# Retention's values and keys through small tiles while attention's room is taken

## The chip, the cores and the metric

The kernel runs on one core of a Trainium2 chip. The metric is the device time of one execution in microseconds (us). The core has a matrix engine (TensorE, PE in the profile; its weight loads stand apart as PEld), VectorE (DVE), ScalarE (ACT), GpSimd (POOL) and a queue that issues transfers (SyncE, SP). Each takes its instructions in the order in which they were written; semaphores tie them together.

## The reference

Two layers of a diffusion backbone over 1024 latent tokens and 256 context tokens, width 1024. What matters of a layer:

```python
h, gate_lat = modulate(x, norm_gain[i], cond_lat @ w_mod[i] + b_mod[i])
(a_uv, a_g, r_q, r_k, r_v, r_g, g_q, g_k, g_v, g_g, s_q, s_k, s_v, s_g) = split_columns(h @ w_in[i])
mlp_l = chunk_mlp_branch(a_uv, a_g, mlp_mix[i], mlp_bias[i])
ry_l, _, _ = retention_bidir(to_heads(r_q), to_heads(r_k) * k_scale, to_heads(r_v), lg_f, lg_b, st_f, st_b)
ret_l = from_heads(rms_norm(ry_l, ret_gain)) * jax.nn.silu(r_g)
ga_l = from_heads(blocked_attention(...)) * jax.nn.silu(g_g)
swa_l = from_heads(window_attention(...)) * jax.nn.silu(s_g)
x = x + gate_lat * (jnp.concatenate([mlp_l, ret_l, ga_l, swa_l], axis=-1) @ w_out[i])
```

Retention works in chunks of 128 tokens: `kv` is the product of decayed keys and values of a chunk, a scan over the chunks makes states of it, and each output is a product inside the chunk plus one with the state before it. The context tokens (two of the ten chunks) go through the same weights, in the second layer only where the latent tokens need them.

## The kernel before, in words

The input projection of a layer is cut into 13 groups of 256 columns, in the order C0, gg, C1, sg, D0, v, D1, ua0, Bv, Bk, Bb0, Bb1, ua1: C and D make queries, keys and values of the two attentions (global and windowed), gg and sg their gates, v and ua the MLP's parts, Bv and Bk retention's values and keys, Bb0 and Bb1 its queries and gates. Four groups of the output projection follow. A group is made of units. `unit_a` (L429) makes two chunks of tokens by 256 columns in 48 matmuls, `unit_b` (L443) 128 columns by four chunks in 24 matmuls of 512 or by two chunks in 24 of 256 (fp32 in three passes of two rounded halves). Each unit writes one PSUM tile of the tag `pj`, of which there are two: a unit can start only when the unit before the last one has been evacuated.

Everything else is hung between the units. While the program is built, a planner keeps a modelled clock of every engine. A step is put down with `later(fn, need, when)`: it is written into the queues when its time has come by the model, when the tiles it needs will be free within 300 ns (`fits`), and when its condition `when` holds. Steps with matmuls come through `pe`. Attention runs as jobs from a list (`attend`, `scores`), at most three in flight: S = q k (L974), the row maximum (DVE, L993), exp (ACT, L1015), a split into two fp16 halves (ACT L1023, DVE and POOL L1032), two transposing DMAs (L1029, L1035), the product with the values (L1045), a sum into M (L1057, L1061), and at the end of a chunk of four token blocks `norm`, which takes a tile of the tag `gd` for the gate and needs it before M can go. When a unit finds no free `pj`, the planner goes on writing only jobs and steps until one comes free (`room`, `until`).

Pools of tiles (`BUFS`, `ATT`): `gd` has 4 tiles of 128x512 f32. Its users near the change are the gate `gt` of an attention chunk and `tab`, the constants for retention's decay tables (`decay_tables`, loaded at L695 and last read at L715). `qkt` has 2 large tiles. They hold the queries and keys of an attention group until the scores of all its jobs are written, and afterwards retention's values (`vt`) and keys (`kT`).

In `ret_v_group` each of the five units of Bv is evacuated by ScalarE into its part of `vt` (L1275). The first of these evacuations waits for a `qkt` tile, the others until that one has taken it. In `ret_k_group` the six units of Bk, two of 256 and four of 512 columns, are evacuated into `kT` with the factor 0.125 (L1293), again the first one waiting for `qkt`. Each is then turned by TensorE into a `pm` tile (`turn`, ktp at L579), scaled by the decay into `kf` (L1314 and L1316, which need `PT` tiles: all three for the first, since two become the states), multiplied with the values (kvp, L1330) and scanned (L1363). Bb0 and Bb1 then make queries and gates; `ready` (sc, L1386) waits until the scan of its half is done and the decay tables are there; `outs` (y, L1414, L1418) follows.

Of the kernel before, what the change touches and what calls it, by code (L numbers as in the profile page):

```python
# [12 lines left out]
F32 = mybir.dt.float32  # L13
# [3 lines left out]
AF = mybir.ActivationFunctionType  # L17
# [5 lines left out]
NT = 10  # L23
# [15 lines left out]
LOOK = 300.0  # L39
# [151 lines left out]
class Program:  # L191
# [161 lines left out]
    def room(self, need):  # L353
        self.until(lambda: self.fits([(need, 1)], None))
# [914 lines left out]

    def ret_v_group(self, W, st):  # L1270

        def keep(pair, ps):
            if "v" not in st:
                st["v"] = self.tile(self.ap, (128, NT, 256), F32, "qkt", "vt")
            self.S.activation(st["v"][:, 2 * pair:2 * pair + 2, :].rearrange("p t c -> p (t c)"), ps, AF.Copy)  # L1275
            self.done(ps)
            st["values"] = st.get("values", 0) + 1

        for pair in (4, 0, 1, 2, 3):
            ps = self.unit_a(W, pair, last=pair == 3)  # L1280
            self.later(lambda pair=pair, ps=ps: keep(pair, ps), "qkt" if pair == 4 else "", None if pair == 4 else lambda: "v" in st)

    def ret_k_group(self, W, st):
        V, S, T, lc = self.V, self.S, self.T, self.lc[self.l]

        kvs, sts = {}, {}
        st["st"], st["S"] = sts, set()

        def get(p, ch, ps):
            t0, n = CHUNKS[ch]  # L1290
            if "k" not in st:
                st["k"] = self.tile(self.ap, (128, 2, NT * 128), F32, "qkt", "kT")
            S.activation(st["k"][:, p, 128 * t0:128 * (t0 + n)], ps[:, :128 * n], AF.Copy, scale=0.125)  # L1293
            self.done(ps)
            self.pe(lambda: turn(p, ch))

        def turn(p, ch):
            t0, n = CHUNKS[ch]
            pk = self.pm("ktp")
            self.turn(pk, st["k"][:, p, 128 * t0:128 * (t0 + n)], n, "k")  # L1300
            first = not st.get("turned")
            st["turned"] = True
            self.later(lambda: scale(p, ch, pk), "PT:3" if first else "PT", None if first else lambda: len(sts) == 2)

        def scale(p, ch, pk):

            n = CHUNKS[ch][1]
            pkv = pk[:, :128 * n].rearrange("p (t h d) -> p t h d", h=2, d=64)
            if not sts:

                for q in range(2):
                    sts[q] = self.tile(self.ap, (128, NT, 2, 64), F32, "PT", "st")
            kf = self.tile(self.ap, (128, 2, 4, 2, 64), F32, "PT", "kf")
            V.tensor_mul(kf[:, 0, :n], pkv, lc["kd"][:, 0, 2 * p:2 * p + 2].unsqueeze(1).unsqueeze(3).to_broadcast([128, n, 2, 64]))  # L1314
            for h in range(2):
                S.activation(kf[:, 1, :n, h, :], pkv[:, :, h, :], AF.Identity, scale=lc["kd"][:, 1, 2 * p + h:2 * p + h + 1], bias=self.zero)  # L1316
            self.done(pk)
            self.pe(lambda: products(p, ch, kf), "pm", lambda: st.get("values") == 5)

        def products(p, ch, kf):  # L1320
            t0, n = CHUNKS[ch]
            vt = st["v"]
            po = self.pm("kvp")
            for i in range(n):
                for fb in range(2):
                    o = 128 * i + 64 * fb

                    for h in range(2):
                        c = 128 * p + 64 * h
                        T.matmul(po[64 * h:64 * h + 64, o:o + 64], kf[:, fb, i, h, :], vt[:, t0 + i, c:c + 64], start=True, stop=True)  # L1330
            self.done(kf)
            self.later(lambda: keep(p, ch, po), "P" if ch == 2 else "", None if ch == 2 else lambda: p in kvs and (p, ch - 1) in kvs)

        fs, bs = [8, 9, 0, 1, 2, 3, 4, 5, 6, 7], [9, 8, 7, 6, 5, 4, 3, 2, 1, 0]

        def keep(p, ch, po):
            t0, n = CHUNKS[ch]
            if ch == 2:
                kvs[p] = self.tile(self.ap, (128, NT, 2, 64), F32, "P", "kv")
                kvs[p, -1] = True  # L1340
            kvs[p, ch] = True
            S.activation(kvs[p][:, t0:t0 + n].rearrange("p t f d -> p (t f d)"), po[:, :128 * n], AF.Copy)
            self.done(po)
            if ch == 2:
                V.memset(sts[p][:, 8, 0], 0.0)
                V.memset(sts[p][:, 9, 1], 0.0)
                scan(p, range(0, 2), range(0, 2))
            elif ch == 0:
                scan(p, range(2, 6), ())
            else:  # L1350
                scan(p, range(6, 9), range(2, 5))
                self.later(lambda: end(p))

        def end(p):
            scan(p, (), range(5, 9))
            self.done(kvs[p])
            self.later(lambda: st["S"].add(p))

        def scan(p, fwd, bwd):
            steps = [(0, fs[s], fs[s + 1]) for s in fwd], [(1, bs[s], bs[s + 1]) for s in bwd]  # L1360
            both = [x for i in range(max(map(len, steps))) for y in steps for x in y[i:i + 1]]
            for fb, a, b in both:
                V.scalar_tensor_tensor(sts[p][:, b, fb, :], sts[p][:, a, fb, :], lc["cd"][:, 2 * p + fb:2 * p + fb + 1],  # L1363
                                       kvs[p][:, a, fb, :], ALU.mult, ALU.add)

        for ch in (2, 0, 1):
            for p in range(2):
                ps = self.unit_b(W, p, ch, p == 1 and ch == 1)
                self.later(lambda p=p, ch=ch, ps=ps: get(p, ch, ps), "qkt" if (p, ch) == (0, 2) else "", None if (p, ch) == (0, 2) else lambda: "k" in st)

    def ret_out_group(self, W, p, st):
        V, S, G, T, lc = self.V, self.S, self.G, self.T, self.lc[self.l]
# [422 lines left out]
```

## Time and profile before

| | us |
|---|---|
| three runs, median | 1315.66 |
| lowest, highest | 1308.14, 1317.33 |
| the profiled execution's own time | 1318.18 |
| its span, first to last instruction | 1316.4 |
| mean granted clock of TensorE, as a share of full speed | 0.987 |

In the windows view a row gives, for one stretch of the span (us from its start), its length, then for PE, PEld, DVE, ACT and POOL the busy time and the number of instructions, then the clock granted to TensorE as a share of full speed, the share of the DMA engines and GB/s. What a PE's busy time leaves of the length is idle. In the timeline a row gives start, duration, engine, line, operation, output and inputs, shape and count; a bracket at its end holds the idle time before it and what ended that. The tile view gives duration as least, median and greatest in ns and the first and last start in us.

### The profile page before, as it was taken

Reading aid. Unit: us, or ns where it says so; the run is one execution under the profiler, and the core shown is the slowest. Engines: PE = TensorE matmul, PEld = TensorE weight load, DVE = VectorE, ACT = ScalarE, POOL = GpSimd, SP = SyncE. Lnnn points to the kernel's source line nnn. Section 1 sums busy time; section 2 is a strip of 40 time slices with the busy share of each in tenths; the row PEclk is TensorE's granted clock in tenths of the full one; section 3 lists DMA queues with packets and bytes.
Section 4 is the critical chain, followed back from the end, with each engine's and each line's share of the span. In section 5 each row is a group of like instructions: output and inputs, shape, how many; then the busy total and the mean of one; then the engine's idle time right before and its main releaser. Section 6 shows DMA issues by size and latency. Waiting matters only on the chain.

```text
span 1316.4 us, 27946 instructions
## 1 busy us (share of the span) xinstructions
PE 1272.4 (97%) x10720; PEld 1121.9 (85%) x10720; DVE 841.8 (64%) x2022; ACT 703.4 (53%) x1467; POOL 610.6 (46%) x616
## 2 busy tenths in 40 slices
PE   6989999999999899999999999999999889999998
PEld 4877878889989788888999978789888778888998
DVE  4765878888897734237225957778898884523522
ACT  3555768777776831235224647667778674213210
POOL 2585855835843213234112486769486422323320
PEclk9999999999999999999999999999999999988999
DMA  9426899799789922163612257997988985105531
GB/s 365 151 77 153 136 203 214 145 201 204 146 164 192 213 75 69 45 190 115 216 33 99 90 142 145 193 196 134 189 170 156 198 162 117 40 21 196 181 112 49
DMA packets 373351, 194.13 MB, mean 147 GB/s; under 512 B 303297, under 2 KB 333665, under 8 KB 372193
## 3 DMA queue, kind: packets, MB, share of 16 engines
q1 hardware_dynamic: 373072, 192.28, 62.6%
q8 instruction: 84, 1.38, 0.4%
q14 instruction: 51, 0.41, 0.1%
q10 hardware_dynamic: 144, 0.07, 0.0%
HBM read 94.63 MB, written 23.74 MB: 90 GB/s over the span
## 4 chain that ended last, share of the span: by engine, by line
PE 79%; DVE 9%; POOL 3%; ACT 3%; issue 3%; DMA 3%; SPq 1%; POOLq 0%; ACTq 0%; DVEq 0%
PE ua L429 32%; PE ub L443 26%; PE S L974 6%; PE O L1045 5%; DVE P L993 2%; PE y L1418 2%; PE y L1414 2%; PE mod L520 1%; POOL rr L567 1%; DMA xt<-in_x 1%; PE u L1714 1%; PE kvp L1330 1%; PE sc L1386 1%; DVE qr L827 1%; DVE L L1032 1%
## 5 line engine op out<-in xcount | busy, mean ns | idle before, releaser
L429 PE MATMUL ua<-w,HT 128*128 128x256 f32 x4128 | 525.2, 285 | 0.4 <-ACT vt L1275 0.4
L429 PEld LDWEIGHTS ua<-w,HT 128*128 128x128 f32 x4128 | 502.8, 191 | 3.8 <-issue 1.7
L443 PE MATMUL ub<-HT,w 128*128 128x512 f32 (+1 forms) x1824 | 402.8, 374 | 4.8 <-ACT kT L1293 2.5
L443 PEld LDWEIGHTS ub<-HT,w 128*128 128x128 f32 x1824 | 311.7, 193 | 63.3 <-ACT kT L1293 3.3
L372 POOL TENSOR_TENSOR w<-raw,w 128x512 fp32r<-128x512 f32 x132 | 185.1, 1413 | 269.3 <-ACT w L370 240.2
L1032 DVE TENSOR_TENSOR L<-P,H 128x1120 f16<-128x1120 f32 (+2 forms) x104 | 143.1, 1376 | 18.2 <-ACT H L1023 16.8
L370 ACT ACTIVATE w<-raw 128x512 fp32r<-128x512 f32 x136 | 83.3, 625 | 109.1 <-PE ua L429 49.2
L993 DVE CUSTOM_DVE_ANT_0 P<-S,zero 128x512 f32<-128x512 f32 (+2 forms) x216 | 116.1, 581 | 29.7 <-PE S L974 14.0
L974 PE MATMUL S<-qkt 128*128 128x256 f16 (+2 forms) x768 | 124.7, 304 | 4.1 <-DVE mx L993 4.1
L1032 POOL TENSOR_TENSOR L<-P,H 128x160 f16<-128x160 f32 (+2 forms) x104 | 81.3, 782 | 97.2 <-ACT H L1023 65.0
L1023 ACT ACTIVATE H<-P 128x1280 f16<-128x1280 f32 (+2 forms) x104 | 124.5, 1197 | 2.1 <-DMA PT<-H 1.2
L1015 ACT ACTIVATE P<-P,mx,gmxC 128x1280 f32<-128x1280 f32 (+1 forms) x72 | 97.5, 1354 | 17.7 <-DVE mx L1002 16.6
L1045 PE MATMUL O<-vh,PT 128*128 128x128 f16 (+1 forms) x1952 | 101.8, 207 | 4.3 <-DVE M L1061 3.1
L974 PEld LDWEIGHTS <-qkt 128*128 128x128 f16 x768 | 64.5, 98 | 45.5 <-issue 7.6
L1045 PEld LDWEIGHTS <-PT 128*128 128x128 f16 x1952 | 88.2, 98 | 14.4 <-issue 8.0
L1598 DVE TENSOR_TENSOR tm<-ua,gb 128x512 f32<-128x512 f32 (+1 forms) x37 | 24.9, 674 | 114.5 <-PE ua L429 114.5
L573 ACT ACTIVATE ev<-ub 128x512 f32<-128x512 f32 (+1 forms) x64 | 34.7, 542 | 110.0 <-PE ub L443 89.7
L567 POOL TENSOR_TENSOR rr<-rt,mhalf 128x6 f32<-128x6 f32 (+3 forms) x60 | 76.2, 1269 | 5.0
L1015 ACT ACTIVATE P<-P,mx,gmxD 128x640 f32<-128x640 f32 (+2 forms) x72 | 61.4, 853 | 16.9 <-DVE mx L1006 12.5
L1121 DVE SCALAR_TENSOR_TENSOR sl<-th,ev 128x512 f32<-128x512 f32 (+1 forms) x40 | 34.4, 860 | 34.5 <-ACT th L1116 32.9
L993 DVE CUSTOM_DVE_ANT_0 P<-S,mask 128x512 f32<-128x512 f32 (+2 forms) x112 | 50.5, 483 | 8.1 <-PE S L974 5.4
L827 POOL TENSOR_TENSOR rt<-sw,cst 128x192 f32<-128x192 f32 x64 | 49.2, 789 | 3.0 <-ACT sw L833 2.6
(177 smaller groups left out, 1547.0 us busy)
## 6 DMA issues: line engine op xcount, KB each, us to landing
raw<-in_win SPq DMA_DIRECT2D x104, 256.0 KB
raw<-in_wmod SPq DMA_DIRECT2D x64, 256.0 KB
wm<-in_wmod SPq DMA_DIRECT2D x8, 1024.0 KB
raw<-in_wout SPq DMA_DIRECT2D x32, 256.0 KB
xt<-in_x SPq DMA_DIRECT2D x4, 1024.0 KB
silu<-sl SPq DMA_DIRECT2D x16, 256.0 KB
gt<-silu SPq DMA_DIRECT2D x16, 256.0 KB
mxd<-mg SPq DMA_DIRECT2D x16, 256.0 KB
```

The source lines that it names most:

```text
L370: self.S.activation(w[:, :, 0, :], rv, AF.Copy)
L372: self.e(f"w{'i' if o < 0 else 'to'[o > 0]}low{q}").tensor_sub(w[:, :, 1, :], rv, w[:, :, 0, :].bitcast(F32))
L429: self.T.matmul(ps[:, 256 * i:256 * i + 256], self.HT[:, 2 * pair + i, k, sa, :], W[k // 2][:, k % 2, sb, :], start=(j == 0 and n == 0), s ...
L443: self.T.matmul(ps[:, :128 * n], W[k // 2][:, k % 2, sa, 128 * b:128 * b + 128], self.HT[:, t0:t0 + n, k, sb, :], start=(k == 0 and m == 0 ...
L567: self.G.tensor_tensor(r[:, :n], t[:, :n], self.mhalf[:, :n], ALU.pow)
L827: E.tensor_mul(out[:, :, :, 32 * c:32 * c + 32], x[:, :, :, 32 * c:32 * c + 32], t.to_broadcast([128, 2, 3, 32]))
L974: T.matmul(sp[o // 4][:, c:c + 128 * m], qk[:, t, heads[s], :], qk[:, keys[i]:keys[i] + m, b, :], start=(b == 2), stop=(b == 3))
L993: V.tensor_tensor_reduce(out=P[:, 128 * o:128 * (o + m)], in0=sp[o // 4][:, c:c + 128 * m], in1=mk, scale=1.0, scalar=-3e38, op0=ALU.add, ...
L1015: S.activation(P[:, ws * s:ws * s + ws], P[:, ws * s:ws * s + ws], AF.Exp, scale=lc["c"][typ][0], bias=mx[:, s:s + 1], accum_out=sv[:, col ...
L1023: S.activation(H[:, 0:w], P[:, 0:w], AF.Copy)
L1032: E.tensor_sub(L[:, a:b], P[:, a:b], H[:, a:b])
L1045: T.matmul(O[:, 128 * s:128 * s + m], pt[:, pl * len(cols) + j, :], vh()[:, kt, 0:m], start=(j % nk == 0 and pl == 0), stop=(j % nk == nk ...
```

## The change

Both groups now ask for their `qkt` tile at once, in a step of its own (`room`). A unit that is done before the tile is there may be evacuated into a `gd` tile ("wait"), if at least two of the four are free at that moment (`spare`); GpSimd then copies it to its place once the large tile has been taken, and frees the small one. Only then does the evacuation count as done: for the values in `st["values"]`, for the keys by starting `turn`. `turn` has a new condition besides: the first waits until three `PT` tiles are free, the others until the states have taken theirs.

```diff
     def ret_v_group(self, W, st):
+        def room():
+            st["v"] = self.tile(self.ap, (128, NT, 256), F32, "qkt", "vt")
+
         def keep(pair, ps):
-            if "v" not in st:
-                st["v"] = self.tile(self.ap, (128, NT, 256), F32, "qkt", "vt")
-            self.S.activation(st["v"][:, 2 * pair:2 * pair + 2, :].rearrange("p t c -> p (t c)"), ps, AF.Copy)
-            self.done(ps)
+            self.evac_or_move(ps, 512, lambda: st["v"][:, 2 * pair:2 * pair + 2, :].rearrange("p t c -> p (t c)"), "v" in st, lambda: "v" in st, 1.0, over)
+
+        def over(src):
             st["values"] = st.get("values", 0) + 1
 
+        self.later(room, "qkt")
         for pair in (4, 0, 1, 2, 3):
             ps = self.unit_a(W, pair, last=pair == 3)
-            self.later(lambda pair=pair, ps=ps: keep(pair, ps), "qkt" if pair == 4 else "", None if pair == 4 else lambda: "v" in st)
+            self.later(lambda pair=pair, ps=ps: keep(pair, ps), "", lambda: "v" in st or self.spare())
+
+    def spare(self):
+        return sum(r <= self.now + LOOK for r in self.slots["gd"]) >= 2
+
+    def evac_or_move(self, ps, n, dst, now, there, factor, then):
+        if now:
+            self.S.activation(dst(), ps[:, :n], AF.Copy, scale=factor)
+            self.done(ps)
+            then(dst())
+            return
+        x = self.gd(n="wait")
+        self.S.activation(x[:, :n], ps[:, :n], AF.Copy, scale=factor)
+        self.done(ps)
+
+        def move():
+            self.G.tensor_copy(dst(), x[:, :n])
+            self.done(x)
+            then(dst())
+
+        self.later(move, "", there)
 
     def ret_k_group(self, W, st):
...
         def get(p, ch, ps):
             t0, n = CHUNKS[ch]
-            if "k" not in st:
-                st["k"] = self.tile(self.ap, (128, 2, NT * 128), F32, "qkt", "kT")
-            S.activation(st["k"][:, p, 128 * t0:128 * (t0 + n)], ps[:, :128 * n], AF.Copy, scale=0.125)
-            self.done(ps)
-            self.pe(lambda: turn(p, ch))
+            self.evac_or_move(ps, 128 * n, lambda: st["k"][:, p, 128 * t0:128 * (t0 + n)], "k" in st, lambda: "k" in st, 0.125,
+                              lambda src: self.pe(lambda: turn(p, ch), "pm", lambda: len(sts) == 2 or not st.get("turned") and self.fits([("PT", 3)], None)))
+
+        def room():
+            st["k"] = self.tile(self.ap, (128, 2, NT * 128), F32, "qkt", "kT")
...
+        self.later(room, "qkt", lambda: "v" in st)
         for ch in (2, 0, 1):
             for p in range(2):
                 ps = self.unit_b(W, p, ch, p == 1 and ch == 1)
-                self.later(lambda p=p, ch=ch, ps=ps: get(p, ch, ps), "qkt" if (p, ch) == (0, 2) else "", None if (p, ch) == (0, 2) else lambda: "k" in st)
+                self.later(lambda p=p, ch=ch, ps=ps: get(p, ch, ps), "", lambda: "k" in st or self.spare())
```

## Rows read from the trace of the kernel before

**Rows 1.** The page's first part: busy time, share of the span, instructions.

```profile
PE 1272.4 (97%) x10720; PEld 1121.9 (85%) x10720; DVE 841.8 (64%) x2022; ACT 703.4 (53%) x1467; POOL 610.6 (46%) x616
```

**Rows 2.** Windows view, the three stretches without projection matmuls and what follows two.

```profile
435.90:448.12 12.22, 7.83 (x104) 5.97 (x101) 10.75 (x41) 10.91 (x26) 2.76 (x5) 1.00 0.95 217
448.12:452.45 4.33, 4.33 (x31) 3.65 (x31) 3.22 (x10) 3.11 (x9) 0.71 (x2) 0.61 0.99 236
1026.13:1039.17 13.04, 8.19 (x111) 6.66 (x109) 11.23 (x40) 9.82 (x25) 4.20 (x5) 1.00 1.04 208
1072.45:1082.97 10.52, 6.92 (x67) 4.90 (x65) 9.96 (x32) 7.23 (x17) 3.83 (x5) 0.84 0.76 157
1082.97:1088.34 5.37, 5.37 (x33) 4.16 (x33) 3.09 (x15) 3.65 (x9) 0.00 (x0) 0.68 0.49 91
```

**Rows 3.** Timeline of PE, layer 0, group Bk.

```profile
435.90 2.36 PE L974 MATMUL S<-qkt 128*128 128x256 f16 x24
...
448.12 2.93 PE L443 MATMUL ub<-HT,w 128*128 128x512 f32 x6 [2.04 <-ACT kT L1293]
...
452.45 1.63 PE L443 MATMUL ub<-HT,w 128*128 128x512 f32 x6
```

**Rows 4.** Timeline of PE, layer 1, group Bv.

```profile
1021.74 4.55 PE L429 MATMUL ua<-w,HT 128*128 128x256 f32 x36
...
1032.61 1.01 PE L1045 MATMUL O<-vh,PT 128*128 128x128 f16 x20 [1.64 <-DVE M L1061]
...
1039.17 3.02 PE L429 MATMUL ua<-w,HT 128*128 128x256 f32 x23 [0.42 <-ACT vt L1275]
```

**Rows 5.** Timeline of PE, layer 1: a block's scores earlier, then group Bk.

```profile
1042.15 1.05 PE L974 MATMUL S<-qkt 128*128 128x256 f16 x8
...
1072.45 2.40 PE L974 MATMUL S<-qkt 128*128 128x256 f16 x24
...
1080.61 1.89 PE L974 MATMUL S<-qkt 128*128 128x256 f16 x8 [0.68 <-DVE mx L993]
1082.97 2.93 PE L443 MATMUL ub<-HT,w 128*128 128x512 f32 x6 [0.47 <-ACT kT L1293]
```

**Rows 6.** Windows view, the long stretches behind the retention groups' start.

```profile
452.45:700.00 247.55, 246.99 (x1931) 221.50 (x1929) 95.11 (x187) 79.64 (x202) 71.86 (x62) 0.99 0.35 107
1090.00:1310.00 220.00, 219.09 (x1649) 196.06 (x1648) 84.30 (x152) 55.33 (x110) 59.41 (x48) 0.97 0.35 106
```

**Rows 7.** Timeline of PE, whole units run together (48 matmuls of 256, 24 of 512).

```profile
1014.20 5.99 PE L429 MATMUL ua<-w,HT 128*128 128x256 f32 x48
...
1138.79 5.75 PE L443 MATMUL ub<-HT,w 128*128 128x512 f32 x24
...
1173.38 8.16 PE L443 MATMUL ub<-HT,w 128*128 128x512 f32 x24
```

**Rows 8.** Decay constants' tile tab in layer 1, tile view: its load, its last reader.

```profile
L715 ACT ACTIVATE qd<-tab,lconst x4: 385/386/386, 1074.8 to 1075.7; 128x128 f32<-128x128 f32 x4
L695 SPq DMA_DIRECT2D tab<-in_consts x1: 570/570/570, 1056.9 to 1056.9; - x1
```

**Rows 9.** Groups by line and shape, POOL: busy us, mean ns, idle before.

```profile
L1136 POOL TENSOR_SCALAR gsq<-gsq 128x512 f32<-128x512 f32 x17 | 12.4, 730 | 14.3 <-ACT gsq L1132 13.3
```

**Rows 10.** Timeline of all engines, layer 1, POOL and DVE side by side.

```profile
1063.86 1.04 POOL L1078 TENSOR_TENSOR M<-M,rs 128x512 f32<-128x512 f32 x1 [0.34 <-DVE rs L1074]
...
1063.98 1.07 DVE L704 SCALAR_TENSOR_TENSOR dec<-tab,lconst,tb 128x128 f32<-128x128 f32 x1
...
1068.32 0.35 DVE L704 SCALAR_TENSOR_TENSOR dec<-tab,lconst,tb 128x128 f32<-128x128 f32 x1
```

**Rows 11.** The keys' tile ktp in layer 0, tile view: DVE's reads of it.

```profile
L1314 DVE TENSOR_TENSOR kf<-ktp,kd x6: 417/682/692, 467.6 to 489.2; 128x512 f32<-128x512 f32 x4, 128x256 f32<-128x256 f32 x2
```

**Rows 12.** Windows view, L443 on PE alone, from Bk's end to the first scores.

```profile
481.30:497.76 16.46, 11.49 (x69) 1.00 0.37 123
...
1116.75:1128.86 12.11, 7.43 (x31) 1.00 0.20 70
```

## The prediction

> **What bounds the kernel now.** I read the page's busy times first. PE is busy for 1272.4 us of the span of 1316.4 us [rows 1], so TensorE bounds the kernel, no change that leaves its work alone can win more than 44.0 us of idle time and what a lowered clock costs, and the question is how much of both lies where this change acts. The timeline of PE shows where projection matmuls stop because both `pj` tiles wait for a large tile. There are three such stretches: Bk in layer 0, where after 435.90 us only attention and small steps run until kT's evacuation lets L443 go on at 448.12 [rows 3]; Bv in layer 1, from the end of a unit at about 1026 until vt's evacuation at 1039.17 [rows 4]; and Bk in layer 1, from 1072.45 to 1082.97 [rows 5]. Bv of layer 0 has no such hole. The windows view gives their price: 12.22 us with 7.83 busy, 13.04 with 8.19, 10.52 with 6.92 [rows 2], so 4.39, 4.85 and 3.60 us idle, 12.84 together. In the same rows DVE is busy for 10.75, 11.23 and 9.96 us, 86 to 95 per cent: there PE waits for attention's chain through DVE and has no projection to put in between. The clock adds to it. Right behind the first stretch TensorE was granted 0.61 of full speed for 4.33 us, and in the third and behind it 0.84 and 0.68 [rows 2]: its lower level of 1.2 GHz for part of these stretches, after PE had stood still in pieces. Six matmuls of L443 took 2.93 us at 448.12 and at 1082.97, and 1.63 us at 452.45 [rows 3, 5]; eight of L974 took 1.89 us against 1.05 [rows 5].
>
> **The change part by part.** *The hole is filled.* The evacuation itself (one ScalarE copy of a unit) stays as it is in number and size; only its target and its moment change. A unit evacuated early frees a `pj` tile, and the next unit takes 5.99 us (L429) or 5.75 us (L443) of PE's time [rows 7]. The first hole needs 4.39 us of such work: one early evacuation in Bk gives one unit of 512 columns, 5.75 us. The two holes of layer 1 hang together: what PE does ahead in the first one is missing before the second, since DVE sets when the scores end. So the second hole must be filled with 4.85 + 3.60 = 8.45 us of Bk's large units: two of them, 11.5 us, that is two `wait` tiles. They are to be had: of four `gd` tiles `tab` holds one, two can be taken by the rule of `spare`, one is left for attention's gate. In Bv three can be taken. So all three holes can be filled, and the idle time gained is at most 12.84 us.
>
> *The clock.* With projections running through, PE doesn't stand still before these places. The loss there, from the granted clock [rows 2], is 4.33 x 0.39 = 1.69 us and 5.37 x 0.32 = 1.72 us, and in the third stretch the scores' 1.89 - 1.05 = 0.84 us [rows 5]: 4.25 us. Bounds: nothing comes back, or all. I take half, 2.1 us, because a row at the lower level far from any hole exists too: 24 matmuls of L443 took 8.16 us at 1173.38 against 5.75 us at 1138.79 [rows 7]; the clock falls in other places than the holes, and nothing here says that it will not fall a little later.
>
> *What is added.* Each early evacuation brings one GpSimd copy of 128x512 (or 128x256). The trace has no such copy; the nearest row is one input to one output of the same size by a tensor-scalar step, 730 ns [rows 9]. Bounds on the path: 0, if no engine waits for it, up to 1.04 us, the GpSimd operation of the same size in rows 10. I expect about seven copies (two or three in each hole and none or one in layer 0's Bv), some 5 us of GpSimd in a whole run where it is busy for 610.6 us [rows 1]. Queued behind a copy is GpSimd's eighth of the split (L1032), for which the transposing DMA and the next product with the values wait, so up to two or three copies' time reaches the end of attention; the projections now beside it hide that on PE. No DMA is added, and nothing on SP's queue moves except with the units' own weight loads. `turn` now waits for three `PT` tiles instead of running ahead and holding a `pm` tile; in the old trace the first kf is made at 467.6 us [rows 11], when the `PT` tiles come free, so the transposes that ran ahead gained nothing beyond one transpose and its wait, which I put at 0.5 us a layer, 1.0 in all, hidden or not (bounds 0 and 2).
>
> *A rule that speaks against it.* While GpSimd's L1078 ran for 1.04 us, DVE's L704, which started 0.12 us later and reads two operands in SBUF, took 1.07 us; by itself it takes 0.35 us [rows 10]. The Trainium skill (SBUF — State Buffer, Who interferes with whom) has a rule for this: a DVE instruction with two SBUF inputs and a GpSimd instruction that reads SBUF exclude each other for the whole instruction. By that rule, and the trace agrees, every copy may hold up DVE's L1032 for up to its own length, in the very stretch that DVE bounds; with three copies of 0.73 us behind layer 1's first hole, an estimate from this page and rows 9, D1's scores would end 2.2 us later and Bk would need 8.45 + 2.2 = 10.65 us of filling, still under 11.5. The sum would stay; its margin would nearly go.
>
> *Where the stall goes.* The gain must survive until the end. Behind the holes PE is busy for 246.99 of 247.55 us and for 219.09 of 220.00 [rows 6], so time won before them is time won at the end, as long as PE finds work. The next late thing is retention's own chain, from the `PT` tiles (467.6) to the first sc (497.76 in layer 0); PE runs Bb0's units meanwhile, 11.49 us of L443 in layer 0 and 7.43 in layer 1 [rows 12]. With 4.4 and 8.45 us more to be covered it needs 15.9 and 15.9 us. From the code, Bb0's queries keep `ga` tiles (4 in all) until sc, and a gate needs two: three queries and two gates can be evacuated and two more units fill `pj`. That is over 28 us in each layer: enough.
>
> *Sum.* 12.84 us idle, less what stays idle where filled attention stretches run (I take 0.8 us), plus 2.1 us of clock, less 1.0 us for the new wait: 13.1 us. The profiled execution's own time is 1318.18 us, 1.8 over its span; less 13.1 it is 1305.1. The median of the runs shown is 2.5 us below that execution, which would make 1302.6. I say 1304.
>
> **The rivals.**
> *The time comes back in retention's chain.* PE runs ahead and then waits for the scan, because `turn` starts later and only one kf fits besides the states. For it: the chain hangs on attention's end, which DVE sets and nothing here moves. Against: the room of 28 us. It would give back all that was won, 1316 to 1318 us, and show as PE waiting in front of ktp, kvp or sc.
> *It doesn't do what it says.* `gt` and `tab` hold two `gd` tiles when a unit wants one, so that only one early evacuation passes in layer 1's Bk, and the plan writes the jobs as sparsely as before. Then the holes of layer 0's Bk and layer 1's Bv are filled, but the latter's 4.85 us comes back in the last one: 4.39 us plus little clock, about 1312.
> *It goes the other way.* The wait tiles starve attention of `gd`. Taken in Bv and Bk they can stand until D's last scores are written; `tab` keeps the fourth from its load at 1056.9 until 1076.1 us [rows 8], 19.2 us. `norm` then has no tile for its gate, M stays, O stays in `pm`, scores stop, and these scores are what the wait tiles wait for, so PE runs dry. It decides from 6.5 us a layer (the 13.1 won); with two thirds of 19.2 us lost in each layer it is 1318.2 - 13.1 + 25.6, about 1330. Against it: `spare` leaves one tile, and M has two buffers.
> *More than the holes.* Three of the low-clock stretches behind retention's y (each 8.16 - 5.75 = 2.4 us in rows 7) fall away because the plan shifts: 7.2 us more, about 1297. As many may come new.
>
> **How the numbers follow.** The forecast 0.58, about half of it below 1302.5; more than the holes 0.10; no effect in layer 1 0.14; given back 0.10, a little of it above 1 per cent slower; starved 0.08. A difference under 1 per cent can't be told from none here, since the three runs lie 9 us apart. Faster by over 1 per cent (below 1302.5) is 0.28 + 0.10 = 0.38; slower by over 1 per cent (above 1328.8) is 0.09; within, 0.53. The range leaves out the low end of the better clock and the starved case: 1293 to 1318. The forecast's own range, with clock and idle at their bounds, is 1300 to 1310.
>
> **What would show it.** Right: in both Bk and in layer 1's Bv, L443 and L429 between the last scores of D0 and D1, PE's idle time in these stretches under 1 us each; evacuations into `wait` before the last scores and copies on POOL of some 0.7 us right behind; PE's busy time unchanged or lower, the span shorter by what its idle time lost; no granted clock near 0.6 behind the holes. Wrong: PE idle before ktp, kvp or sc (given back), before S or O with DVE idle too (starved), or before L443 with kT as releaser (not filled). Fewer than two copies in a Bk group, or an idle sum that doesn't fall by 10 us, makes the prediction wrong.

## The result and the profile after

The changed kernel took 1300.11 us (median of four runs, 1296.89 to 1307.29) against 1316.49 us: a ratio of 0.9892, 95% interval 0.9861 to 0.9922. Two later measurements of the same kernel gave 0.9874 (0.9856 to 0.9893) and 0.9876 (0.9851 to 0.9901). So it is 1.1 to 1.3 per cent faster, some 16 us. The profiled execution took 1298.90 us. Its page answers [rows 1]:

```profile
span 1297.1 us, 27962 instructions
PE 1262.1 (97%) x10720; PEld 1114.6 (86%) x10720; DVE 840.1 (65%) x2022; ACT 703.7 (54%) x1467; POOL 614.1 (47%) x626
```

The ten more instructions on POOL are the copies. PE does the same 10720 matmuls in 10.3 us less busy time, and its idle time, span less busy, fell from 44.0 to 35.0 us. Both halves need an explanation: less waiting, and a higher clock. The windows view shows the waiting. First the changed kernel, whose layer 1 begins some 6 us earlier:

```profile
380.00:520.00 140.00, 138.70 (x1283) 120.47 (x1282) 87.08 (x271) 77.83 (x182) 45.43 (x46) 1.00 0.66 142
1000.00:1060.00 60.00, 60.00 (x605) 56.77 (x604) 47.34 (x139) 41.62 (x93) 27.19 (x27) 1.00 0.90 175
1060.00:1100.00 40.00, 36.40 (x310) 29.29 (x309) 31.11 (x103) 29.03 (x67) 11.82 (x14) 0.96 0.84 159
1000.00:1130.00 130.00, 126.40 (x1198) 110.23 (x1197) 93.36 (x287) 83.55 (x187) 45.03 (x45) 0.99 0.74 150
```

and the kernel before over the same long stretches:

```profile
380.00:520.00 140.00, 134.55 (x1257) 117.60 (x1256) 89.05 (x275) 75.21 (x179) 42.05 (x41) 0.99 0.64 134
1000.00:1130.00 130.00, 120.93 (x1186) 105.19 (x1183) 99.25 (x303) 86.28 (x192) 44.74 (x41) 0.97 0.76 151
```

Layer 0's idle time went from 5.45 to 1.30 us, layer 1's from 9.07 to 3.60: 9.6 us together. Layer 1's Bv is closed (60.00 of 60.00 us busy), and what is left stands between 1060 and 1100. The timeline of PE of the changed kernel shows where the first hole was [rows 3] and what is left of the last [rows 5]:

```profile
435.81 1.26 PE L974 MATMUL S<-qkt 128*128 128x256 f16 x12
436.82 4.36 PE L443 MATMUL ub<-HT,w 128*128 128x512 f32 x18
...
441.88 1.26 PE L974 MATMUL S<-qkt 128*128 128x256 f16 x12
442.90 1.64 PE L443 MATMUL ub<-HT,w 128*128 128x512 f32 x6
...
1068.69 1.64 PE L443 MATMUL ub<-HT,w 128*128 128x512 f32 x6
1070.17 1.02 PE L1045 MATMUL O<-vh,PT 128*128 128x128 f16 x20
...
1071.50 1.26 PE L974 MATMUL S<-qkt 128*128 128x256 f16 x12
...
1075.06 0.97 PE L1045 MATMUL O<-vh,PT 128*128 128x64 f16 x19 [2.24 <-DMA PT<-L]
1075.86 5.05 PE L974 MATMUL S<-qkt 128*128 128x256 f16 x32
1081.51 1.65 PE L443 MATMUL ub<-HT,w 128*128 128x512 f32 x6 [0.60 <-ACT wait L1298]
```

In layer 0 units of L443 now stand between the scores, each at full speed (1.64 us for six). In layer 1 no matmul of a unit starts from 1070.2 to 1081.5, and PE stands idle for 2.24 and 0.60 us there. The tile view of `wait` in that stretch says why, with the line of `tab`'s last reader from its own view:

```profile
L1298 ACT ACTIVATE wait<-ub x3: 384/385/573, 1049.9 to 1080.9; 128x256 f32<-128x256 f32 x2, 128x512 f32<-128x512 f32 x1
...
L715 ACT ACTIVATE qd<-tab,lconst x4: 384/386/386, 1078.6 to 1079.4; 128x128 f32<-128x128 f32 x4
```

Two small units were taken early; the third, a large one, only at 1080.9, 1.1 us after `tab`'s last reader had ended (1079.4 + 0.39). Over the whole kernel ten units went through small tiles: one and three in layer 0, three and three in layer 1.

For the clock I added (1 - granted clock) x 5 us over windows of 5 us, up to the last window in which PE works: an estimate of the time that a stretch lost to the lower level, too high where PE also stood idle. Idle time and this loss, in us, for all kernels of this study:

| profile of | span | idle: layer 0, 380 to 520 | idle: layer 1, 1000 to 1130 | clock loss in these two | clock loss, 520 to 700 and from 1130 |
|---|---|---|---|---|---|
| before | 1316.4 | 5.5 | 9.1 | 5.2 | 8.5 |
| values alone | 1318.3 | 5.5 | 11.2 | 6.9 | 8.5 |
| no small tiles | 1318.3 | 5.6 | 7.8 | 5.1 | 6.8 |
| keys alone | 1301.7 | 1.1 | 3.6 | 1.8 | 8.5 |
| changed, three profiles | 1297.1, 1297.1, 1294.6 | 1.3, 1.1, 1.7 | 3.6, 2.9, 3.4 | 1.7, 2.2, 1.7 | 3.4, 6.3, 2.0 |
| copies on VectorE | 1301.2 | 0.9 | 4.7 | 0.0 | 10.2 |
| last tile too | 1295.9 | 0.8 | 2.0 | 0.0 | 5.1 |
| late tables, two | 1291.0, 1297.8 | 2.1, 1.5 | 0.3, 0.3 | 0.0, 2.5 | 1.7, 7.7 |
| late and last, two | 1292.6, 1293.4 | 0.7, 2.3 | 2.1, 2.1 | 0.0, 0.0 | 5.2, 5.1 |

In the two attention stretches the changed kernel won 9.6 us of idle time and 3.5 us of clock, 13.1 us. The last column, the stretches with retention's outputs, differs by 5.1 us more between the first profiles of the two kernels; together that is 18.2 of the 19.3 us between their spans. But this column goes from 2.0 to 6.3 us in three profiles of the one changed kernel, and from 1.7 to 7.7 in two of another.

### The profile page after: what moved, and what is told of

Same layout as the page of the kernel before. It is cut to its first block, busy times and chain, and to the rows that moved or that the text cites. A ratio compares the mean times of both kernels' runs of the same rounds, so it can differ in the third digit from the quotient of the medians.

```text
span 1297.1 us, 27962 instructions
## 1 busy us (share of the span) xinstructions
PE 1262.1 (97%) x10720; PEld 1114.6 (86%) x10720; DVE 840.1 (65%) x2022; ACT 703.7 (54%) x1467; POOL 614.1 (47%) x626
## 5 line engine op out<-in xcount | busy, mean ns | idle before, releaser
L443 PE MATMUL ub<-HT,w 128*128 128x512 f32 (+1 forms) x1824 | 397.3, 370 | 2.9 <-ACT ev L573 1.8
L443 PEld LDWEIGHTS ub<-HT,w 128*128 128x128 f32 x1824 | 306.7, 190 | 58.3 <-issue 2.9
L372 POOL TENSOR_TENSOR w<-raw,w 128x512 fp32r<-128x512 f32 x132 | 189.0, 1441 | 288.6 <-ACT w L370 259.8
L1032 DVE TENSOR_TENSOR L<-P,H 128x1120 f16<-128x1120 f32 (+2 forms) x104 | 146.6, 1410 | 19.0 <-ACT H L1023 19.0
L974 PE MATMUL S<-qkt 128*128 128x256 f16 (+2 forms) x768 | 125.2, 305 | 0.0
L1032 POOL TENSOR_TENSOR L<-P,H 128x160 f16<-128x160 f32 (+2 forms) x104 | 76.3, 735 | 88.6 <-ACT H L1023 56.8
L1045 PE MATMUL O<-vh,PT 128*128 128x128 f16 (+1 forms) x1952 | 101.8, 207 | 3.9 <-DMA PT<-L 3.8
L974 PEld LDWEIGHTS <-qkt 128*128 128x128 f16 x768 | 65.0, 99 | 41.8 <-issue 6.1
L1045 PEld LDWEIGHTS <-PT 128*128 128x128 f16 x1952 | 87.4, 98 | 15.0 <-issue 7.6
```

Of the source, the lines that this page charges most:

```text
L372: self.e(f"w{'i' if o < 0 else 'to'[o > 0]}low{q}").tensor_sub(w[:, :, 1, :], rv, w[:, :, 0, :].bitcast(F32))
L443: self.T.matmul(ps[:, :128 * n], W[k // 2][:, k % 2, sa, 128 * b:128 * b + 128], self.HT[:, t0:t0 + n, k, sb, :], start=(k == 0 and m == 0 ...
L974: T.matmul(sp[o // 4][:, c:c + 128 * m], qk[:, t, heads[s], :], qk[:, keys[i]:keys[i] + m, b, :], start=(b == 2), stop=(b == 3))
L1032: E.tensor_sub(L[:, a:b], P[:, a:b], H[:, a:b])
L1045: T.matmul(O[:, 128 * s:128 * s + m], pt[:, pl * len(cols) + j, :], vh()[:, kt, 0:m], start=(j % nk == 0 and pl == 0), stop=(j % nk == nk ...
```

## The experiments

**The halves.** Three kernels: Bk as before, with only the values through small tiles; Bv as before, with only the keys; and everything but the small tiles.

```diff
 # no small tiles
     def spare(self):
-        return sum(r <= self.now + LOOK for r in self.slots["gd"]) >= 2
+        return False
```

Values alone (`ret_k_group` of the kernel before), expected:

> Only Bv goes through small tiles; Bk is as before (its first evacuation waits for the large tile, its transposes run ahead). Theory H (the holes: the time won is PE's idle time where projections stood still, and the clock behind it): layer 1's Bv hole (4.85 us idle) closes, but TensorE then reaches layer 1's Bk hole earlier and most of it comes back there; layer 0's Bk hole (4.39 us and the clock behind it) stays as it was. 0 to 4 us faster than before, PE idle in all 40 to 44 us. Rival P (the plan behind the new order of the transposes, or fewer low-clock stretches by chance, brings the gain, not the holes): the new condition of the transposes isn't here, so 0 too if it is the transposes; 8 us or more if any new plan does it.

Measured: 1317.46 us, ratio 1.0027 (1.0012 to 1.0042), slightly slower; the page's idle time is 48.2 us. Both lie outside what was expected (0 to 4 us faster, 40 to 44 us idle). Of the 4.2 us more idle time than before, 2.1 stand in the first 100 us, which the change doesn't touch. Bv's hole is gone, and Bk's has grown, as its timeline of PE shows:

```profile
1055.92 3.11 PE L443 MATMUL ub<-HT,w 128*128 128x256 f32 x24
...
1065.21 1.35 PE L1045 MATMUL O<-vh,PT 128*128 128x64 f16 x15 [3.06 <-DMA PT<-L]
...
1071.93 0.84 PE L1045 MATMUL O<-vh,PT 128*128 128x128 f16 x16 [2.39 <-DVE mx L993]
...
1079.39 1.67 PE L1045 MATMUL O<-vh,PT 128*128 128x64 f16 x19 [2.95 <-DMA PT<-L]
...
1086.64 1.68 PE L443 MATMUL ub<-HT,w 128*128 128x512 f32 x6 [0.47 <-ACT kT L1318]
```

No unit from 1059 to 1086.6; PE idles 11.2 us between 1000 and 1130, 2.1 more than before. So in this kernel closing a hole ahead of another one that waits for the same thing moved the time and won none.

Keys alone (`ret_v_group` of the kernel before), expected:

> Only Bk goes through small tiles; Bv is as before. Theory H: layer 0's Bk hole closes (4.39 us idle, some 1.7 us of clock), layer 1's Bk hole (3.60 us idle, some 2.6 us of clock) closes for the most part, layer 1's Bv hole (4.85 us idle) stays: 8 to 12 us faster than before, PE idle 34 to 38 us. Rival P: if it is the new order of the transposes, the whole gain of some 16 us is here.

Measured: 1302.31 us, ratio 0.9914 (0.9891 to 0.9938). That is 0.86 per cent, 11 us, in the expected range, and more than two thirds of the whole. Its 3.6 us of idle time in layer 1 are Bv's hole, still there (an idle stretch of 1.65 us before L1045 at 1028.91, as in [rows 4]); both Bk holes are filled.

No small tiles, expected:

> The change without its small tiles: the large tile is asked for at once and the transposes wait for their PT tiles, but no unit is ever evacuated into a wait tile. Theory H: all three holes stay, 0 to 2 us from before either way, PE idle 43 to 45 us. Rival P (the pm tiles that the waiting transposes no longer hold let attention end sooner): 6 us or more faster.

Measured: 1316.80 us, ratio 1.0014 (0.9994 to 1.0035); idle 47.0 us in all, 2 more than expected, and that much stands in the first 100 us, which the change doesn't touch. So asking early for the large tile and delaying the transposes win nothing by themselves: the rival falls.

The changed kernel beside them, expected:

> The changed kernel as it is, beside the three others on one chip. Both theories: 0.985 to 0.992 of before, some 1300 us; PE idle about 35 us in the profiled execution. Theory H wants the sum of the gains of the two halves (values alone, keys alone) to be below this one, since the holes of layer 1 hang together.

Measured: 1298.92 us, ratio 0.9874. Values alone lose 0.3 per cent and keys alone win 0.9, and the two together win 1.3: values pay only once the keys can take over the time they win.

**What is left in layer 1.** Four kernels, each one edit on the changed one.

```diff
 # late tables
-                self.later(lambda: self.decay_tables(l), "gd vf vh")
+                self.later(lambda: self.decay_tables(l), "gd vf vh", lambda: "k" in st)
 # last tile too
-        return sum(r <= self.now + LOOK for r in self.slots["gd"]) >= 2
+        return sum(r <= self.now + LOOK for r in self.slots["gd"]) >= 1
 # copies on VectorE
-            self.G.tensor_copy(dst(), x[:, :n])
+            self.V.tensor_copy(dst(), x[:, :n])
 # late and last: the first two, and this part of turn's condition for the first transpose
-not st.get("turned") and self.fits([("PT", 3)], None)
+not st.get("turned") and not self.jobs and not self.flight and self.fits([("PT", 3)], None)
```

Late tables, expected:

> The changed kernel, but the decay tables (which hold a gd tile from their load until their last reader) are asked for only once the keys have their large tile. In the changed kernel layer 1's Bk still shows 2.8 us of idle PE and a lowered clock between 1071 and 1082 us; a third small tile is taken only at 1080.9, just after the tables let theirs go. Theory H: with that tile free the third evacuation comes some 8 us earlier, a large unit (5.75 us) fills the rest of the hole, and the tables' work on DVE (4 times 0.28 + 0.35 us) leaves the stretch that DVE bounds: 3 to 6 us faster than the changed kernel, 0.983 to 0.985 of before. Rival: the hole's end is set by DMA and DVE alone and PE has enough to do; or the tables now come late for the first scores: no gain, or 1 to 3 us slower than the changed kernel.

Measured: 1298.04 us, ratio 0.9868 (0.9840 to 0.9896). In the profile the step did what was said. The third unit's evacuation came at 1062.7 instead of 1080.9, and the hole is gone, as the windows view shows:

```profile
1000.00:1130.00 130.00, 129.74 (x1197) 114.09 (x1196) 90.90 (x268) 83.70 (x184) 49.08 (x50) 1.00 0.75 149
```

So with `tab`'s tile free the third unit passed. The same edit also takes the tables' work on DVE out of this stretch (its first instruction comes at 1085.6 us instead of 1065.7), so this run alone doesn't separate the two; the next one does. The span was 1291.0 us. The median, though, isn't apart from the changed kernel's ratio, where 3 to 6 us were expected.

The last tile too, expected:

> The changed kernel, but a unit may take the last free gd tile too (one free instead of two). Theory H: the third unit of layer 1's Bk is evacuated as soon as the gate's tile comes free, and the rest of the hole closes: 2 to 5 us faster than the changed kernel. Rival S (starving, the prediction's third rival): attention's norm finds no tile for its gate, M and O stay, the scores that would free the large tile come late: 5 us or more slower than the changed kernel, with PE idle before L974 or L1045 in one of the three places.

Measured: 1299.38 us, ratio 0.9874 (0.9849 to 0.9899). Nothing starved: PE's one new wait on M is 0.59 us, at 1086.52. Here `tab` was loaded at 1060.0 us (1062.3 in the changed kernel), and still the third unit was evacuated at 1064.0; so it was the missing tile, by `tab` and the rule of two together, that kept it out. The idle time in layer 1 is 2.0 us, 1.26 of it just before L443 goes on at 1082.36 us. Eleven units went through small tiles instead of ten. The time is that of the changed kernel, not the 2 to 5 us less that were expected.

Copies on VectorE, expected:

> The changed kernel with the ten copies from the small tiles on VectorE instead of GpSimd. Theory H: VectorE bounds attention there, ten copies of some 0.4 us delay its end by at most 4 us in all, in stretches where PE now has other work: within 2 us of the changed kernel, slower rather than faster. Rival (GpSimd's copies hold VectorE up through the shared port for their own length, so that it is the better place): 1 to 3 us faster than the changed kernel.

Measured: 1300.62 us, ratio 0.9885 (0.9864 to 0.9906), the same within what can be told. Which engine copies made no difference to the time that these runs can show.

Late and last together, expected:

> The two together: late tables and the last gd tile for a unit, the first transpose waiting besides until no attention job is left. Theory H: as with the late tables alone, or up to 2 us better: some 0.982 to 0.985 of before. Rival S: with the last tile taken norm starves: 3 us or more slower than with the late tables alone.

Measured: 1296.26 us, ratio 0.9853 (0.9830 to 0.9877), just above the expected range.

**The best two again**, beside the changed kernel on one chip.

> The changed kernel once more, as the measure for the next two on the same chip: 0.986 to 0.990 of before. PE idle in layer 1 between 1000 and 1130 us 2.5 to 4 us; the clock's loss there under 2 us, and behind retention's outputs anything from 2 to 11 us, since that changes from execution to execution.

Measured: 1299.08 us, ratio 0.9876.

> The late tables again. Theory H: layer 1's remaining hole is closed (idle between 1000 and 1130 us under 1 us, no low clock there), worth 3 to 5 us: 0.982 to 0.987 of before, below the changed kernel beside it. Rival: the clock behind retention's outputs moves by as much from one execution to the next, and no difference from the changed kernel can be told.

Measured: 1298.06 us, ratio 0.9868 (0.9840 to 0.9896). Layer 1's hole is closed again (0.3 us idle), but the clock cost 7.7 us behind retention's outputs in this profile and 1.7 in the first one, so that the spans of one and the same kernel are 1297.8 and 1291.0 us. For the medians the rival is right: the 3 us of the hole drown in this.

> Late tables with the last gd tile for a unit, again. Theory H: as the late tables alone, within 2 us; the last tile adds nothing, since the hole is closed already. Rival: it is the better of the two by 2 us or more, as the first time.

Measured: 1294.64 us, ratio 0.9837 (0.9814 to 0.9860), the fastest of all kernels here, both times ahead of the late tables alone, here by 3.4 us where at most 2 were expected. The intervals of the ratios still overlap a little with the changed kernel's, but all six runs (1291.52 to 1295.73 us) lie under the five of the changed kernel beside them (1296.37 to 1302.88). Why it is ahead is open: its idle time in layer 1 is 2.1 us, more than with the late tables alone. It differs in two ways from these (the last tile, and a first transpose that waits for attention's last job), which weren't separated.

**The same runs at the same clock.** Much of what hides the small differences is the clock. Call a run's span times (1 - mean granted clock) its loss to the clock. Over the 123 runs with a recorded clock, each kernel of each measurement with a level of its own, a straight line fitted to them gives 0.68 us more span for 1 us more of this loss, and the rest scatters by 1.4 us. Read off this line at a loss of 10 us, an estimate good to some 0.5 to 0.8 us (standard error), the spans are:

| kernel | span at a loss of 10 us |
|---|---|
| before, on three chips | 1311.5, 1311.4, 1311.1 |
| values alone; no small tiles | 1312.6; 1311.9 |
| keys alone | 1300.0 |
| changed, three measurements | 1298.1, 1297.6, 1298.8 |
| copies on VectorE; last tile too | 1297.8; 1297.8 |
| late tables, two measurements | 1295.6, 1295.8 |
| late and last, two measurements | 1294.0, 1294.3 |

So the change is worth 12 to 14 us at the same clock, and the keys alone 11.5 us. The late tables win some 2.5 us more, about what the hole had left, and late and last another 1.5 us.

## Why the prediction was right, point by point

**The number.** I forecast 1304 us within 1293 to 1318; it is 1300.11, at the low end of the forecast's own 1300 to 1310. Three of my own signs failed all the same, two by little: the idle time fell by 9.6 us in the two stretches (9.0 in the whole span) where I had called less than 10 a sign of being wrong, layer 1's Bk kept 2.84 us of it where I had asked for under 1, and the clock granted behind that hole was 0.66 from 1075 to 1080 us.

**The bound and the holes.** Right. The waits [rows 2 to 5] were where the time was: with the small tiles switched off nothing is won, with them 16 us. That layer 1's two holes hang together was right too, and the run with the values alone shows it at its plainest.

**The filling.** Right for layer 0's Bk and layer 1's Bv; too good for layer 1's Bk. The step that failed is that two large units, 11.5 us, would do there, because "DVE sets when the scores end". DVE sets it only as long as PE serves it at once. From the first matmul of Bv in layer 1 to the end of attention's last scores it took 70.7 us before and 70.2 us without small tiles, but 75.2 us with the values alone, 75.1 us with the keys alone and 75.4 us after, each time with the same 144 matmuls of L974. The units that now run early stand in PE's queue ahead of scores, and DVE waits for these scores. Its waits for them in that stretch, before and then after:

```profile
DVE P L993 <- PE S L974: 3.1, 1, 3.1
```

```profile
DVE P L993 <- PE S L974: 6.3, 4, 2.5
```

With the values alone these waits are 5.2 us. With the keys alone they are only 3.9, and DVE is busy for 65.52 us of its stretch against 62.14 before, so there PE's queue is not the whole delay. The windows view shows the same as the waits, over the first 40 us from Bv's first matmul on, before and then after:

```profile
1011.82:1051.82 40.00, 35.15 (x390) 33.09 (x388) 36.50 (x113) 29.51 (x66) 16.55 (x15) 1.00 1.00 199
```

```profile
1005.49:1045.49 40.00, 40.00 (x421) 39.18 (x419) 32.05 (x96) 27.41 (x59) 17.09 (x17) 1.00 0.98 188
```

PE won 4.85 us in these 40, and DVE did 4.45 us less. So a third large unit was needed, and `tab` kept it out until 1080.9. Idle time won: 9.6 us instead of 12.0.

**The clock.** Right that it gives something back, and the size was low: I took half of 4.25 us, 2.1, and these stretches gave back 3.5. With the late tables, where layer 1's Bk has no hole, the loss between 1000 and 1130 us is 0.0 both times. But a hole needn't lower the clock, and the clock falls without one: the copies on VectorE left 4.7 us idle in layer 1 with no loss, the kernel without small tiles lost nothing behind layer 0's hole, and its 1.7 us of loss in layer 0, like the 2.5 us of the late tables' second profile, stand from 515 to 520 us, where PE was busy all 5.00 us. So the mechanism is shown in part only. The clock elsewhere, for which I kept the other half back, stands in the table's last column and follows no edit of this study clearly.

**The new wait and the copies.** I charged 1.0 us for the later transposes. They start later, the first kf at 477.0 us instead of 467.6 [rows 11] and the first sc in layer 0 at 506.9 instead of 497.76 [rows 12], and PE found work all that time: from 453.75 to 600 us it is busy for 145.49 of 146.25. So no price is seen, here or in the kernel without small tiles, which has the later transposes too, and the rival by which the time comes back in retention's chain falls; the room in `ga` and `pj` was enough. The copies took 0.40 (256 columns) and 0.61 us (512), where I had bounded them by 0 and 1.04 and named 0.73; one took 1.56, as told below. Ten came instead of seven.

**The rule on the shared port.** The exclusion is there, but in the other direction than I feared. In the timeline at the end of attention in layer 1 POOL's copies wait and DVE doesn't:

```profile
1081.54 1.31 DVE L1032 TENSOR_TENSOR L<-P,H 128x1120 f16<-128x1120 f32 x1
```

```profile
1081.54 2.47 POOL L1302 COPY kT<-wait 128x256 f32<-128x256 f32 x3
```

DVE's split took 1.31 us, its usual time (the median of all 104 is 1.33); of the three copies behind one another the first, which began with the split, took 1.56 us instead of 0.40 (tile view). The Trainium skill (SBUF — State Buffer, Who interferes with whom) says that a DVE instruction with two SBUF inputs contends with a GpSimd instruction that reads SBUF, and that this is an exclusive lock; the 1.2 us by which this copy is longer, near the split's 1.31 us, agree. Other work of GpSimd does hold the split: beside L1078, which ran from 1044.48 to 1045.53 us right behind three copies, the split begun at 1044.66 took 2.04 us. Copies moved to VectorE leave the time as it is.

**Starving** didn't come, even where a unit may take the last `gd` tile. **The sum** came out at 13.1 us in the attention stretches, as I had it, from other parts: 9.6 + 3.5 + 0 for 12.0 + 2.1 - 1.0. That the totals agree is luck: an idle gain that was too high met a clock gain that was too low and a price that didn't come. The medians differ by 16.4 us. The remaining 3 us fit a lower clock loss behind retention's outputs (6.8 to 8.5 us in the three kernels without keys through small tiles, 1.7 to 10.2 with them); these ranges overlap, so it isn't shown that the change brings it. I put the chance of more than 1 per cent at 0.38 and of less at 0.53; it is just above 1 per cent.

## What to carry to other kernels

A hole in the bounding engine that is caused by a missing place to put results can be worth less than its idle time, if a later hole waits for the same event; look for that one first, and give it the spare tiles. Work that fills a hole goes into an in-order queue ahead of the work that would end the hole, so count it twice: as time won, and as delay of the chain. And ask who else holds tiles of the small pool just then; here a table that could be made later kept out the one unit that was missing.

## What the runs showed of the hardware

The lowered clock of TensorE costs this kernel about as much as its holes, and less steadily: in profiles of the same instructions the loss behind retention's small matmuls was 2.0 to 6.3 us (changed) and 1.7 and 7.7 (late tables). It falls there while PE has no idle time: in the changed kernel's profile PE is busy for all 5.00 us of each window from 1140 to 1165, yet the granted clock is 1.00 up to 1155 and then 0.79 and 0.87, and eight of retention's output matmuls (L1444) take 1.08 us at 1157.79 where they took 0.66 us just before. In the changed kernel's four runs the time follows the mean granted clock: 1296.89 us at 0.997, 1298.90 at 0.993, 1301.31 at 0.990 and 1307.29 at 0.984. In this kernel a difference of a few us between single runs says nothing before that clock has been looked at; read at the same loss to the clock, three measurements of one kernel came within 1.2 us of each other.
